# A state buffer with time as its outermost axis, in the S5 recurrence of a hybrid layer

## The chip, the cores and the metric

The kernel runs on one core of one Trainium2 chip. The metric is the device time of one execution in microseconds, with its inputs in the chip's memory. Times of the profile are in microseconds unless marked ns.

## The reference, cut to what matters

The kernel computes one whole layer on 256 tokens of width 2048 in fp32: a mixer with three branches (gated delta rule, gated linear attention, S5 state space model), a cross-attention and a convolutional feed-forward part. The change touches the S5 branch alone. It has 64 groups with 64 complex states each, that is 4096 complex states, and runs them over 256 steps of time:

```
bu_r = jnp.einsum('bsgh,gph->sbgp', uf, bbr)
bu_i = jnp.einsum('bsgh,gph->sbgp', uf, bbi)
...
_, _, xr, xi = lax.associative_scan(combine, (a_r, a_i, bu_r, bu_i), axis=0)
y = (jnp.einsum('sbgp,ghp->bsgh', xr, c_re.astype(f32))
     - jnp.einsum('sbgp,ghp->bsgh', xi, c_im.astype(f32)))
y = y + d_skip.astype(f32).reshape(S5_GROUPS, S5_GROUP) * uf
```

The scan is the recurrence x(t) = a x(t-1) + b u(t) with a complex factor a for each state. The output is a product of all states with C, plus a skip term.

## The kernel before, in words

**The work as a whole.** TensorE multiplies the 256 tokens by all weight matrices, in fp32 split into a high and a low part. The helper `load_w` (line 199) fetches a weight group of 128 x 1024 values, lets ScalarE round it to its high part `whi` and VectorE subtract to get the low part `wlo` (both line 206). `proj` (line 229) and `proj_tok` (line 269) then issue three matmuls for each piece (lines 212 to 221 and 285 to 287), into PSUM accumulators from a pool of five; `total` (line 223) adds the two halves of an accumulator, by a ScalarE copy (L225) and a VectorE add (L226), and so frees it for the next slab.

**The order of the work.** The small stages (the S5 recurrence, the delta rule `dn_core`, the gated linear attention `gla_core`) are Python generators. After each weight group `pump` (line 148) advances the active generators by as much as their rates (R_S5 = 0.7, R_DN = 1.15, R_GLA = 1.7) allow; each `yield` names the share that the piece issued so far uses up. So the instructions of several stages are interleaved in each engine's queue, and each engine works its queue in order. Weight splits have a higher priority than the rest.

**The S5 core** (`s5_core`, line 905) works in two halves of 128 steps of time. The tile X holds, on each of 128 partitions, the real and imaginary part (axis c, 2) of 32 states (axis n) at 128 times (axis s): 8192 words, with time as the innermost axis. Each half has three stages:

- The input products: 64 fp32 matmuls (line 922; each is recorded twice, once for each pass) into PSUM tiles from a pool of three, and 16 evictions by ScalarE (line 926) of 128 x 512 values into X.
- The recurrence on VectorE: for each time t a multiply of the previous states, X[:, :, :, t - 1], by the tile M of factors, into `mm` (line 932, 128 values a partition), an add of the two parts of `mm` into `s_` (line 933, 64 values), and an add of `s_` to X[:, :, :, t] in place (line 934, 64 values). In the first half the first time needs no step, so there are 255 steps. Between the halves the last state is copied into the tile `carry` (line 937), which the first step of the second half reads.
- The output products: 64 fp32 matmuls (line 947; again each recorded twice) with the columns of C as weights and X[:, c, n, :], 128 times, as the moving operand; four of them, for four blocks of 32 output rows, go to four column groups of the array. VectorE and ScalarE then apply skip term and GELU (lines 953 to 961).

In profile lines the tile s_ appears as s__868, and f names tiles of the shared pools; su, the S5 input, is one of them.

**Where it lies in time.** The first half's evictions run from 120 to 161 us, its steps from 161 to 465, its output products from 485 to 494. The second half's evictions run from 487 to 564, its steps from about 565 to 821, its output products from 853 to 869. In the same stretches lie the projections of the mixer with the delta rule (to about 490 us) and the gated linear attention (540 to 660 us).

Of the kernel before, what the change touches and what calls it, by code (L numbers as in the profile page):

```python
# [9 lines left out]
F32 = mybir.dt.float32  # L10
# [8 lines left out]
P = 128  # L19
# [69 lines left out]
class Net:  # L89
# [350 lines left out]
    def dn_core(self):  # L440
# [76 lines left out]
        for i in range(1, 32):  # L517
            tv = tmp[:64, :i * i].rearrange("p (c j) -> p c j", c=i)
            nc.vector.tensor_mul(tv, X3[:64, :i, :i], LS[:64, :i, i][:, None, :].broadcast_to([64, i, i]))  # L519
            nc.vector.tensor_reduce(X3[:64, :i, i], tv, axis=AX.X, op=ALU.add)  # L520
            yield 0.14 + i * i * 2 / 960.0
# [295 lines left out]
    def s5_setup(self, brT, biT):  # L817
# [5 lines left out]
        def tl(n):  # L823
            return self.scr()
        self.X = None
        self.side.dma_start(out=self.Bl[0], in_=brT)
# [78 lines left out]
    def s5_core(self, ctr, cti):  # L905
        nc = self.nc
        su = self.su
        carry = self.s5s.tile([P, 2, 32], F32, name="carry")
        m = self.s5s.tile([P, 2, 2, 32], F32, name="mm")
        s = self.s5s.tile([P, 2, 32], F32, name="s_")  # L910
        for hf in range(2):
            X = self.s5p.tile([P, 2, 32, P], F32, name="X", tag="X")
            tk = slice(hf * P, hf * P + P)
            for f2 in range(4):
                for q2 in range(0, 4, QB):
                    pss = [self.mx([P, 2, 2, P]) for _ in range(QB)]
                    for n in range(2):
                        ft = 2 * f2 + n
                        for c in range(2):
                            for q, ps in enumerate(pss, q2):  # L920
                                rs = slice(32 * q, 32 * q + 32)
                                nc.tensor.matmul(ps[:, n, c, :], self.Bl[c][rs, ft, :], su[rs, ft, tk], start=True,  # L922
                                                 stop=True, tile_position=(32 * q, 0))
                    for q, ps in enumerate(pss, q2):
                        p0 = 8 * f2 + q
                        nc.scalar.copy(X[:, :, p0:p0 + 5:4, :].rearrange("p c n s -> p n c s"), ps)  # L926
                    yield 1.0 * QB
            for t in range(P):
                if t == 0 and hf == 0:
                    continue  # L930
                prev = carry if t == 0 else X[:, :, :, t - 1]
                nc.vector.tensor_mul(m, self.M, prev[:, None].broadcast_to([P, 2, 2, 32]))  # L932
                nc.vector.tensor_add(s, m[:, :, 0, :], m[:, :, 1, :])  # L933
                nc.vector.tensor_add(X[:, :, :, t], X[:, :, :, t], s)  # L934
                yield 0.48
            if hf == 0:
                nc.vector.tensor_copy(carry, X[:, :, :, P - 1])
            Ct = [self.tile4().rearrange("p (n o) -> p n o", n=32) for _ in range(2)]
            self.side.dma_start(out=Ct[0], in_=ctr)
            self.side.dma_start(out=Ct[1], in_=cti)  # L940
            for fb in range(2):
                ps = self.mx([P, 4, P])
                for f in range(4):
                    ft = 4 * fb + f
                    for c in range(2):
                        for q in range(4):
                            nc.tensor.matmul(ps[32 * q:32 * q + 32, f, :], Ct[c][:, 4 * ft + q, :],  # L947
                                             X[:, c, 4 * ft + q, :], start=(c == 0), stop=(c == 1),
                                             tile_position=(0, 32 * q))
                sv = su[:, 4 * fb:4 * fb + 4, tk]  # L950
                for f in range(4):
                    ft = 4 * fb + f
                    nc.vector.scalar_tensor_tensor(sv[:, f, :], sv[:, f, :], self.vec[:, V_S5D + ft:V_S5D + ft + 1],
                                                   ps[:, f, :], op0=ALU.mult, op1=ALU.add)
                y2 = self.tile4(512).rearrange("p (f s) -> p f s", f=4)
                nc.scalar.activation(y2, sv, AF.Square)
                nc.vector.tensor_scalar(y2, y2, 0.044715, 1.0, op0=ALU.mult, op1=ALU.add)
                nc.vector.tensor_mul(y2, y2, sv)
                nc.scalar.activation(y2, y2, AF.Tanh, scale=GELU_C)
                nc.vector.tensor_scalar(y2, y2, 1.0, None, op0=ALU.add)  # L960
                nc.vector.tensor_mul(sv, sv, y2)
                yield 3.0
# [612 lines left out]
```

## Time and profile before

| what | value |
|---|---|
| median of 3 runs | 1946.44 us (1944.46 to 3108.89) |
| the profiled execution | 1944.89 us |
| its span, first to last instruction | 1943.1 us |
| granted TensorE clock, mean | 0.991 |
| instructions | 28177 |

The profile is of one execution. Busy times of the engines overlap. TensorE's matmuls are pipelined, and each record is longer than the time until the next one starts; an idle time in brackets after a row is that before its first instruction, with what ended it.

### The profile page before, as it was taken

To read this page: it belongs to the slowest core of one execution; us is meant where nothing else is said; L and a number is where in the kernel's file an instruction comes from. 1 tells how busy PE (TensorE), PEld (TensorE's weight loads), DVE (VectorE), ACT (ScalarE), POOL (GpSimd) and SP (SyncE) were. 2 spreads that over 40 slices of the span, in tenths; PEclk is the share of its full clock that TensorE was granted. 3 is DMA by queue.
4 is the path that set the end of the run, shared out by engine and by line. 5 is a ranking of instruction groups with operands and counts; after the bars stand their busy time and mean duration, and the time that the engine had idled before them with its cause. 6 is when DMAs were issued, how large, how long until landed. Compare 5 with 4: busy or idle time off the path is not lost.

```text
span 1943.1 us, 28177 instructions
## 1 busy us (share of the span) xinstructions
PE 1881.5 (97%) x10440; PEld 1567.1 (81%) x10440; DVE 1419.6 (73%) x2719; ACT 952.3 (49%) x1426; POOL 67.4 (3%) x117
## 2 busy tenths in 40 slices
PE   7989899999999999999999997999999999999997
PEld 6778788777778688878877986888888888888886
DVE  6868999996569999967666856766666666644445
ACT  5655444343564444544454655555555555534442
POOL 0000012020000000000000000000000000000000
PEclk9999999999999999999999998999999999999999
DMA  7535467674445576666576544655566555676664
GB/s 250 175 108 171 147 205 237 187 260 132 125 126 165 180 220 180 213 216 207 184 262 214 176 147 147 215 185 174 184 195 188 188 187 185 202 226 200 199 192 135
DMA packets 107482, 363.93 MB, mean 187 GB/s; under 512 B 12320, under 2 KB 20896, under 8 KB 106832
## 3 DMA queue, kind: packets, MB, share of 16 engines
q1 hardware_dynamic: 97696, 328.32, 54.9%
q0 software_dynamic: 9648, 33.81, 5.2%
q8 instruction: 82, 1.34, 0.3%
q14 instruction: 56, 0.46, 0.1%
HBM read 350.47 MB, written 11.61 MB: 186 GB/s over the span
## 4 chain that ended last, share of the span: by engine, by line
PE 87%; DVE 7%; issue 4%; DMA 1%; ACT 1%; POOL 0%; SPq 0%; DVEq 0%; ACTq 0%; POOLq 0%
PE acc L218 25%; PE acc L219 14%; PE acc L287 13%; PE acc L285 13%; PE acc L286 13%; DVE wlo L206 2%; PE acc L221 2%; PE mx L922 2%; DVE f L519 1%; DVE mm L932 1%; PE mx L183 0%; PE mx L947 0%; PE mx L641 0%; DVE f L520 0%; DMA mch<-in 0%
## 5 line engine op out<-in xcount | busy, mean ns | idle before, releaser
L206 DVE TENSOR_TENSOR wlo<-raw,whi 128x1024 fp32r<-128x1024 f32 (+1 forms) x632 | 752.8, 1194 | 419.9 <-ACT whi L206 417.6
L206 ACT CAST whi<-raw 128x1024 fp32r<-128x1024 f32 (+1 forms) x632 | 646.7, 1029 | 728.7 <-PE acc L286 378.6
L218 PE MATMUL acc<-aa,whi 128*128 128x512 f32 x2085 | 727.1, 401 | 11.6 <-DVE r L226 9.6
L219 PE MATMUL acc<-aa,wlo 128*128 128x256 f32 x2224 | 556.2, 284 | 10.2 <-DVE wlo L206 10.2
L219 PEld LDWEIGHTS acc<-aa,wlo 128*128 128x128 f32 x2224 | 422.6, 190 | 54.6 <-DVE wlo L206 22.1
L218 PEld LDWEIGHTS acc<-aa,whi 128*128 128x128 f32 x2085 | 386.6, 190 | 82.5 <-issue 11.8
L285 PE MATMUL acc<-whi,aa 128*128 128x512 f32 (+1 forms) x704 | 269.8, 384 | 0.0
L286 PE MATMUL acc<-whi,aa 128*128 128x512 f32 (+1 forms) x704 | 268.5, 382 | 0.0
L287 PE MATMUL acc<-wlo,aa 128*128 128x512 f32 (+1 forms) x704 | 253.3, 385 | 3.7 <-DVE wlo L206 3.6
L287 PEld LDWEIGHTS acc<-wlo,aa 128*128 128x128 f32 x704 | 131.9, 188 | 34.0 <-DVE wlo L206 7.7
L286 PEld LDWEIGHTS acc<-whi,aa 128*128 128x128 f32 x704 | 132.4, 188 | 26.4 <-issue 1.1
L285 PEld LDWEIGHTS acc<-whi,aa 128*128 128x128 f32 x704 | 132.3, 188 | 26.1 <-issue 1.2
L285 PE MATMUL acc<-whi,ach 128*128 128x512 f32 x352 | 136.9, 389 | 0.0
L286 PE MATMUL acc<-whi,acl 128*128 128x512 f32 x352 | 136.9, 389 | 0.0
L287 PE MATMUL acc<-wlo,ach 128*128 128x512 f32 x352 | 123.4, 389 | 0.0
L932 DVE TENSOR_TENSOR mm<-M,X 128x128 f32<-128x128 f32 x254 | 98.6, 388 | 5.4 <-ACT X L926 0.6
L286 PEld LDWEIGHTS acc<-whi,acl 128*128 128x128 f32 x352 | 66.1, 188 | 13.7
L285 PEld LDWEIGHTS acc<-whi,ach 128*128 128x128 f32 x352 | 66.1, 188 | 13.7
L287 PEld LDWEIGHTS acc<-wlo,ach 128*128 128x128 f32 x352 | 66.0, 188 | 13.7
L934 DVE TENSOR_TENSOR X<-X,s__868 128x64 f32<-128x64 f32 x255 | 71.4, 280 | 4.5
L933 DVE TENSOR_TENSOR s__868<-mm 128x64 f32<-128x64 f32 x255 | 56.4, 221 | 4.7
L226 DVE TENSOR_TENSOR r<-r,acc 128x256 f32<-128x256 f32 x143 | 56.9, 412 | 0.7 <-ACT r L225 0.6
(454 smaller groups left out, 1866.9 us busy)
## 6 DMA issues: line engine op xcount, KB each, us to landing
raw<-in SPq DMA_DIRECT2D x600, 512.0 KB, 4.0
raw<-in SPq DMA_DIRECT2D x32, 256.0 KB, 2.7
gd<-r POOLq DMA_DIRECT2D x24, 256.0 KB, 4.5
f<-gd POOLq DMA_DIRECT2D x12, 512.0 KB, 4.9
f<-Rd POOLq DMA_DIRECT2D x4, 512.0 KB, 6.9
f<-in POOLq DMA_DIRECT2D x4, 512.0 KB, 3.7
gp<-in POOLq DMA_DIRECT2D x8, 256.0 KB, 4.5
xn<-in POOLq DMA_DIRECT2D x1, 2048.0 KB, 10.3
```

Source lines behind the costliest of these rows:

```text
L206: self.last = (nc.scalar.copy(hi, raw), self.seq(lambda: nc.vector.tensor_sub(lo, raw, hi.bitcast(F32))))
L218: nc.tensor.matmul(two, hi, x, start=start, stop=False)
L219: nc.tensor.matmul(two[:, 0, :], lo, x[:, 0, :], start=False, stop=False)
L221: nc.tensor.matmul(two, hi, x, start=start, stop=True)
L226: self.nc.vector.tensor_add(r, r, acc[:, 0:T])
L285: nc.tensor.matmul(accs[t], xh[:, ts_], hi[:, kk, :], start=(kt == 0), stop=False)
L286: nc.tensor.matmul(accs[t], xl[:, ts_], hi[:, kk, :], start=False, stop=False)
L287: last[:] = [nc.tensor.matmul(accs[t], xh[:, ts_], lo[:, kk, :], start=False, stop=(kt == KT - 1))]
L922: nc.tensor.matmul(ps[:, n, c, :], self.Bl[c][rs, ft, :], su[rs, ft, tk], start=True, stop=True, tile_position=(32 * q, 0))
L932: nc.vector.tensor_mul(m, self.M, prev[:, None].broadcast_to([P, 2, 2, 32]))
L933: nc.vector.tensor_add(s, m[:, :, 0, :], m[:, :, 1, :])
L934: nc.vector.tensor_add(X[:, :, :, t], X[:, :, :, t], s)
```

## The change

X is allocated with time as its outermost free axis: [time, part, state] in place of [part, state, time]. The number of words, the pool and the buffer stay. Every access to X is rewritten for the new layout: the evictions write it through a permuted view, the recurrence reads and writes X[:, t], and the output products read X[:, :, c, n]. The numbers, order and arithmetic of the instructions in the program text and the amounts that each `yield` names are the same.

```diff
-            X = self.s5p.tile([P, 2, 32, P], F32, name="X", tag="X")
+            X = self.s5p.tile([P, P, 2, 32], F32, name="X", tag="X")
...
-                        nc.scalar.copy(X[:, :, p0:p0 + 5:4, :].rearrange("p c n s -> p n c s"), ps)
+                        nc.scalar.copy(X[:, :, :, p0:p0 + 5:4].rearrange("p s c n -> p n c s"), ps)
...
-                prev = carry if t == 0 else X[:, :, :, t - 1]
+                prev = carry if t == 0 else X[:, t - 1]
                 nc.vector.tensor_mul(m, self.M, prev[:, None].broadcast_to([P, 2, 2, 32]))
                 nc.vector.tensor_add(s, m[:, :, 0, :], m[:, :, 1, :])
-                nc.vector.tensor_add(X[:, :, :, t], X[:, :, :, t], s)
+                nc.vector.tensor_add(X[:, t], X[:, t], s)
...
-                nc.vector.tensor_copy(carry, X[:, :, :, P - 1])
+                nc.vector.tensor_copy(carry, X[:, P - 1])
...
-                                             X[:, c, 4 * ft + q, :], start=(c == 0), stop=(c == 1),
+                                             X[:, :, c, 4 * ft + q], start=(c == 0), stop=(c == 1),
```

## Rows read from the trace of the kernel before

**Rows 1.** The page, busy time, share of the span and instructions of each engine.
```profile
PE 1881.5 (97%) x10440; PEld 1567.1 (81%) x10440; DVE 1419.6 (73%) x2719; ACT 952.3 (49%) x1426; POOL 67.4 (3%) x117
```
**Rows 2.** The page, the chain that ended last, by engine and by line.
```profile
PE 87%; DVE 7%; issue 4%; DMA 1%; ACT 1%; POOL 0%; SPq 0%; DVEq 0%; ACTq 0%; POOLq 0%
PE acc L218 25%; PE acc L219 14%; PE acc L287 13%; PE acc L285 13%; PE acc L286 13%; DVE wlo L206 2%; PE acc L221 2%; PE mx L922 2%; DVE f L519 1%; DVE mm L932 1%; PE mx L183 0%; PE mx L947 0%; PE mx L641 0%; DVE f L520 0%; DMA mch<-in 0%
```
**Rows 3.** Windows: stretch and length, busy time by engine, clock, DMA share, GB/s.
```profile
core 0: us, PE busy (x) PEld busy (x) DVE busy (x) ACT busy (x) POOL busy (x), PEclk, DMA share, GB/s
100.00:161.00 61.00, 55.73 (x351) 47.36 (x351) 41.59 (x84) 32.98 (x54) 0.00 (x0) 0.94 0.43 128
161.00:300.00 139.00, 132.54 (x722) 112.00 (x721) 132.41 (x331) 68.39 (x101) 7.73 (x11) 0.99 0.58 175
363.00:400.00 37.00, 33.36 (x141) 25.68 (x140) 37.00 (x47) 13.62 (x14) 1.66 (x4) 1.00 0.63 191
570.00:600.00 30.00, 26.59 (x270) 22.14 (x270) 29.24 (x60) 13.41 (x22) 0.00 (x0) 0.89 0.43 132
660.00:822.00 162.00, 162.00 (x819) 134.32 (x818) 154.44 (x378) 77.84 (x110) 6.89 (x12) 1.00 0.67 208
```
**Rows 4.** TensorE's waits for VectorE (total, times, longest): 161-300, 300-465, 465-600 us.
```profile
PE acc L218 <- DVE r L226: 4.4, 5, 1.6
...
PE mx L398 <- DVE f L393: 2.1, 1, 2.1
...
PE acc L287 <- DVE wlo L206: 3.6, 6, 1.3
...
PE acc L218 <- DVE r L226: 2.0, 1, 2.0
...
PE acc L218 <- DVE s__868 L933: 1.4, 1, 1.4
```
**Rows 5.** The recurrence's groups of instructions, then L932's form that reads the carry tile.
```profile
L932 DVE TENSOR_TENSOR mm<-M,X 128x128 f32<-128x128 f32 x254 | 98.6, 388 | 5.4 <-ACT X L926 0.6
L934 DVE TENSOR_TENSOR X<-X,s__868 128x64 f32<-128x64 f32 x255 | 71.4, 280 | 4.5
L933 DVE TENSOR_TENSOR s__868<-mm 128x64 f32<-128x64 f32 x255 | 56.4, 221 | 4.7
...
L932 DVE TENSOR_TENSOR mm<-M,carry x1: 293/293/293, 465.1 to 465.1; 128x128 f32<-128x128 f32 x1
```
**Rows 6.** Windows of L932 alone: stretch and length, VectorE busy (steps), clock, DMA.
```profile
161.00:171.20 10.20, 2.32 (x6) 1.00 0.35 103
188.90:197.80 8.90, 1.91 (x5) 1.00 0.39 117
215.50:226.50 11.00, 1.90 (x5) 1.00 0.32 93
324.00:396.40 72.40, 7.22 (x19) 1.00 0.64 196
568.00:586.00 18.00, 0.73 (x2) 0.89 0.48 147
```
**Rows 7.** The output products: all of L947, then TensorE's timeline: start, us, instructions.
```profile
L947 PE MATMUL mx<-X,f x256: 272/273/297, 485.2 to 868.5; 128*32 128x128 f32 x128
...
490.87 3.27 PE L947 MATMUL mx<-X,f 128*32 128x128 f32 x112
494.07 0.50 PE L287 MATMUL acc<-wlo,aa 128*128 128x512 f32 x1
```
**Rows 8.** Two VectorE instructions of the delta rule with a strided source.
```profile
L524 DVE COPY f<-f 64x1024 f32<-64x1024 f32 x1 | 1.1, 1117 | 0.0
...
L519 DVE TENSOR_TENSOR f<-f,f 64x961 f32<-64x961 f32 x1 | 1.9, 1935 | 0.0
```
**Rows 9.** ScalarE's evictions: all of L926, then its timeline before the first step.
```profile
L926 ACT COPY X<-mx x32: 567/586/591, 120.3 to 563.3; 128x512 f32<-128x512 f32 x32
...
159.55 1.70 ACT L926 COPY X<-mx 128x512 f32<-128x512 f32 x3 [0.16 <-PE mx L922]
```

## The prediction

> **What bounds the kernel now.** I read the busy shares first, then the chain that ended last, then both by stretch. TensorE is busy for 1881.5 of 1943.1 us, VectorE for 1419.6 [rows 1]; the chain is 87% PE and 7% DVE, and the recurrence's multiply is in it with 1%, L947 with 0% [rows 2]. The average hides that VectorE is nearly full while the recurrence runs: 132.4 us of 139 from 161 to 300, all 37 us from 363 to 400, 29.2 of 30 from 570 to 600, 154.4 of 162 from 660 to 822 [rows 3]. In the last of these TensorE is busy for all 162 us too, so there the full VectorE holds nobody up. So the question is not how much VectorE work the change removes but how long TensorE stands still for VectorE. The waits answer it: from 161 to 300 it waits 4.4 us for L226 (the sum that frees an accumulator) and 2.1 us for L393; from 300 to 465, 3.6 us for weight splits (L206); from 465 to 600, 2.0 us for L226 and 1.4 us for a recurrence step [rows 4]. Together 13.5 us. That is the most that a faster recurrence can return by the waits, however much VectorE time it saves.
>
> **The recurrence's steps.** Their number, order and arithmetic stay; only the step between elements changes, from 512 bytes (128 words) to 4. The multiply L932 takes 388 ns where it reads X, and 293 ns in the one execution that reads the contiguous carry tile, with the same shape: 95 ns is the price of the strided read. The add L934 reads and writes X strided and takes 280 ns; L933, with the same 64 elements and contiguous output, takes 221 ns: 59 ns [rows 5]. So VectorE is spared 254 x 95 + 255 x 59 ns = 24.1 + 15.0 = 39 us, 154 ns a step. The lower end is 0 (only one row shows the contiguous form), the upper 48 us, if L934 pays the 95/128 ns an element on its read and again on its write and so loses 95 ns too. I take 39, the rows' own differences.
>
> **What of that reaches the end.** A wait of TensorE becomes shorter by the steps that VectorE runs since it last had to wait itself, since what is saved before such a wait is lost in it. At the slab ends at 171, 197 and 226 us, VectorE's last own wait lies at most 11 us back (the stretches in rows 6 begin at those waits); 6, 5 and 5 steps lie in those run-ups. Between 324 and 396 it never waits, and 19 steps lie there. Before the waits at 580 and 586 only 2 do; the dense work there is that of the gated linear attention [rows 6]. At 154 ns a step this is 0.9 + 0.8 + 0.8 + 2.9 + 0.3 = 5.7 us, each part below the wait that it shortens. The ends are 0 (other waits take their place) and 13.5 us (all of [rows 4]). From 570 to 600 the granted clock is 0.89 [rows 3]: part of the stretch runs at the lower of the two levels, 1.2 GHz, which costs about 0.11 x 30 = 3.3 us against 2.4 GHz; the engine had stood still for VectorE before that. If the shorter wait spares it that, 3.3 us more are gained; I leave it out of the sum and in the range. From 600 to 870 I cost the gain at nothing: TensorE is full there without the recurrence being late for it.
>
> **The output products, L947.** This is the new cost, and it stands on the path. The moving operand X[:, c, n, :] was 128 contiguous words; now each word lies 256 bytes from the one before. In the trace 112 matmuls start at 490.87 and the next matmul at 494.07 [rows 7]: four run side by side on the four column groups, so 28 groups take 3.20 us, 114 ns a group, 0.89 ns a column. All 256 are 64 groups, some 7.3 us now. No row shows a TensorE read at such a step. The lower end is 0. It isn't idle talk: a VectorE copy with one source read at a 128-byte step does 1024 elements in 1117 ns [rows 8], 1.09 ns each, not far above TensorE's 0.89, so a reader of one stream at this pace may lose little. The upper end by the same kind of rows is that the four streams of a group are fetched in turn, each with the multiply's 95 ns: 256 x 95 = 24.3 us. The nearest row by access is the multiply itself [rows 5]: 128 elements, one strided stream, 95 ns more. Taken once for each group of four (they have run side by side so far) it gives 64 x 95 = 6.1 us, all exposed: the matmuls before and after these blocks follow without a gap and nothing else runs in their place. I take 6.1.
>
> The Trainium skill (Advanced Engine Details and Errata, SBUF Cachelines) says that successive accesses in one 16-byte line run at full rate and that one line per access is penalised. The multiply's 388 against 293 ns agrees for VectorE; for TensorE no run here shows it. By that rule the lower end of 0 falls away, without a size. The Trainium skill (Vector Engine (DVE) Microarchitecture Reference, Measured stream behaviour) gives 1.73 ns an element for far hops and 2.50 for a step of 24 words, against 1.054; as an estimate from that page, TensorE at the larger price would pay 64 x 128 x 1.45 ns = 11.9 us in place of 6.1, and the sum would be 1952.
>
> **The evictions, L926.** 32 ScalarE copies of 512 elements from PSUM, 586 ns each, now write at a step of 256 bytes. Nearest row for an element priced by its stride: 95 ns / 128 = 0.74 ns; so up to 0.38 us each, 12 us of ScalarE in all, and 0 at the lower end. ScalarE is busy for 33.0 of the 61 us in which the first half's evictions lie [rows 3] and is 1% of the chain [rows 2]; its idle time hides nearly all of it. Not hidden is the end of the first half: three evictions stand back to back at 159.55 [rows 9], the first recurrence step waits for the last of them, and behind that step in VectorE's queue wait L226 and the splits that the slab end at 171 needs. I take 3 x 0.38 = 1.1 us, ends 0 and 2. In the second half the last eviction starts at 563.3 [rows 9] and the steps only some 5 us later. The carry copy and the buffers' size don't change, and there is no DMA in the change.
>
> **The sum,** against the profiled execution's own 1944.89 us (span 1943.1 and 1.8 around it; the median of the runs shown, 1946.44, is 1.6 above): -5.7 + 6.1 + 1.1 = +1.5, so 1946.4 us. No change that could be measured.
>
> **Rivals.**
> (a) TensorE reads the steps as fast as contiguous words. For it: a column takes 0.89 ns and the strided one-stream copy 1.09. Against it: the 95 ns of the multiply. Then -5.7 + 0 + 1.1, 1940.3 us, chance 0.28.
> (b) Slower: the four side-by-side streams of L947 share one path into the array and pay in turn, 24.3 us, in blocks whose neighbours follow them without a gap. For it: four streams at once ask for four words in 0.89 ns, which one word per access makes four accesses. Against it: with contiguous words the four show no queueing that the trace would tell, and the multiply's price was measured for one stream. -5.7 + 24.3 + 1.1 gives 1964.6 us. It decides from the point where a group costs over 72 ns more (4.6 us for the 64), since then the gain is gone. Chance 0.18.
> (c) The same, but each access at the whole 1.9 to 2.0 ns an element that the two-source multiply L519 with a strided operand shows (1935 ns for 961 [rows 8]): 4 x 128 x 1.9 = 0.97 us a group in place of 0.114, 64 x 0.86 = 55 us, 1995 us. Chance 0.05.
> (d) The whole 39 us reaches the end, since VectorE is the true limit wherever it is full: 1944.89 - 39 + 7.2 = 1913 us. Against it: rows 3 and 4, 13.5 us of waits. Chance 0.04. A little over 2% needs all of it and a free L947.
> (e) The multiply stays at 388 ns, because the cost lies in the broadcast of its operand and not in the stride: then only costs are left, 1952 us. Against it: the carry row has the same broadcast. Chance 0.03.
> The forecast itself has 0.42.
>
> **How the numbers follow.** 1946.4 is the likeliest case. The range takes in (a) with the larger gain of the waits and of the clock, down to 1932, and (b), up to 1966; (c), (d) and the far ends lie outside. Two per cent are 39 us, about what a measurement of this kernel can tell from no change: only (d) comes near that on the fast side, 0.03, only (c) and a dearer (b) on the slow side, 0.06, and 0.91 stays within.
>
> **What would show it.** L932 near 293 ns, L934 near 221, VectorE's busy time near 1380 us: the first step right. TensorE's waits for VectorE down from 13.5 to about 8 us: the second. A group of L947 at about 209 ns: the third; at 114 it is (a), near 494 (b). L926 at up to 965 ns without TensorE waiting for L926: the fourth. It is wrong if another order of instructions comes out of the build, or if a wait for L926 or X stands where L226 stood.

## The result, and the profile after

The changed kernel takes 1957.65 us (median of 4 runs, 1956.75 to 1960.56) against 1945.45 before (median of 4): ratio 1.0068, 95% interval [1.0055, 1.0082], some 13 us slower. One of the four runs before took 3108.89 us; the ratio leaves it out. The forecast was 1946.4 and no change; the time lies between the forecast and rival (b). The instructions stand in the same order on every engine in both kernels, so each difference of time comes from how long instructions take and who waits.

The page after: busy time, and the chain by engine and by line.
```profile
PE 1897.4 (97%) x10440; PEld 1576.4 (81%) x10440; DVE 1395.9 (71%) x2719; ACT 982.2 (50%) x1426; POOL 67.4 (3%) x117
...
PE 85%; DVE 7%; issue 4%; DMA 2%; ACT 2%; POOL 0%; DVEq 0%; SPq 0%; ACTq 0%; POOLq 0%
PE acc L218 24%; PE acc L219 13%; PE acc L287 13%; PE acc L285 13%; PE acc L286 13%; DVE wlo L206 2%; PE acc L221 2%; PE mx L922 1%; PE mx L947 1%; DMA raw<-in 1%; DVE f L519 1%; PE mx L183 1%; ACT whi L206 0%; PE mx L641 0%; DVE f L520 0%
```
Against [rows 1, 2], VectorE is busy 24 us less, ScalarE 30 us and TensorE 16 us more (VectorE's saving is 40 us and the evictions' price 16; the last section has the rest). L932 has left the list of the chain's lines, and L947 has come up from 0% to 1%. That is the whole story in small: a cost on an engine that was seldom waited for was exchanged for one on the engine that sets the end.

The recurrence's groups after, the counterpart of [rows 5].
```profile
L932 DVE TENSOR_TENSOR mm<-M,X 128x128 f32<-128x128 f32 x254 | 73.2, 288 | 6.5 <-ACT X L926 1.8
L934 DVE TENSOR_TENSOR X<-X,s__868 128x64 f32<-128x64 f32 x255 | 56.4, 221 | 4.5
```
The multiply falls by 100 ns and the add by 59: 25.4 + 15.0 = 40 us of VectorE time.

TensorE's waits for VectorE after (total, times, longest), from 161 to 300, 300 to 465 and 465 to 600 us, the counterpart of [rows 4].
```profile
PE acc L218 <- DVE X L934: 2.6, 2, 1.4
...
PE mx L398 <- DVE f L393: 1.7, 1, 1.7
...
PE acc L218 <- DVE r L226: 1.1, 3, 0.6
...
PE acc L287 <- DVE wlo L206: 2.4, 4, 1.1
...
PE acc L218 <- DVE s__868 L933: 2.2, 1, 2.2
...
PE acc L218 <- DVE r L226: 1.9, 1, 1.9
```
They come to 11.9 us where they were 13.5. Of 40 us saved on VectorE, 1.6 us show in these waits. The rows understate it, since each of TensorE's records is longer than the time until the next one starts, so that an idle stretch shows only a part of a delay. Measured by the start of the same matmul, the first 16 of the output products begin at 480.41 us in place of 485.19. Of these 4.8 us, 1.5 were there at 161 us, before the first step, so the steps gave back 3.3. A stretch where an engine is full is no stretch where it is waited for.

The output products after, in TensorE's timeline (start, us, instructions), the counterpart of [rows 7].
```profile
487.68 10.66 PE L947 MATMUL mx<-X,f 128*32 128x128 f32 x112
498.27 0.51 PE L287 MATMUL acc<-wlo,aa 128*128 128x512 f32 x1
...
876.01 5.94 PE L947 MATMUL mx<-X,f 128*32 128x128 f32 x62
881.88 0.50 PE L285 MATMUL acc<-whi,aa 128*128 128x512 f32 x1
```
The block of 112 begins 3.2 us earlier than before (487.68 against 490.87) and ends 4.2 us later (498.27 against 494.07). 28 groups now take 10.59 us, 378 ns each, where they took 114. By the end of the last block the lead has become a lag of 13.2 us: in the kernel before, the matmul after it started here.
```profile
866.83 1.95 PE L947 MATMUL mx<-X,f 128*32 128x128 f32 x62
868.70 0.50 PE L285 MATMUL acc<-whi,aa 128*128 128x512 f32 x1
```
The span's end lies 13.2 us later too (1956.3 against 1943.1); after 882 us nothing more is lost or gained on balance.

The evictions after, ScalarE's timeline and then VectorE's before the first step, the counterpart of [rows 9].
```profile
158.01 2.91 ACT L926 COPY X<-mx 128x512 f32<-128x512 f32 x3 [0.15 <-PE mx L922]
...
160.95 0.29 DVE L932 TENSOR_TENSOR mm<-M,X 128x128 f32<-128x128 f32 x1 [1.84 <-ACT X L926]
```
Three evictions take 2.91 us in place of 1.70, and the first step waits 1.84 us for the last of them. In [rows 5] all waits of L932 for L926 were 0.6 us.

### The profile page after: what moved, and what is told of

The parts are those of the page before. It is cut to its first block, busy times and chain, and to the rows that moved or that the text cites. A ratio compares the mean times of both kernels' runs of the same rounds, so it can differ in the third digit from the quotient of the medians.

```text
span 1956.3 us, 28177 instructions
## 1 busy us (share of the span) xinstructions
PE 1897.4 (97%) x10440; PEld 1576.4 (81%) x10440; DVE 1395.9 (71%) x2719; ACT 982.2 (50%) x1426; POOL 67.4 (3%) x117
## 4 chain that ended last, share of the span: by engine, by line
PE 85%; DVE 7%; issue 4%; DMA 2%; ACT 2%; POOL 0%; DVEq 0%; SPq 0%; ACTq 0%; POOLq 0%
PE acc L218 24%; PE acc L219 13%; PE acc L287 13%; PE acc L285 13%; PE acc L286 13%; DVE wlo L206 2%; PE acc L221 2%; PE mx L922 1%; PE mx L947 1%; DMA raw<-in 1%; DVE f L519 1%; PE mx L183 1%; ACT whi L206 0%; PE mx L641 0%; DVE f L520 0%
## 5 line engine op out<-in xcount | busy, mean ns | idle before, releaser
L206 ACT CAST whi<-raw 128x1024 fp32r<-128x1024 f32 (+1 forms) x632 | 662.6, 1054 | 723.0 <-PE acc L286 366.5
L932 DVE TENSOR_TENSOR mm<-M,X 128x128 f32<-128x128 f32 x254 | 73.2, 288 | 6.5 <-ACT X L926 1.8
L934 DVE TENSOR_TENSOR X<-X,s__868 128x64 f32<-128x64 f32 x255 | 56.4, 221 | 4.5
```

The source lines that it names most:

```text
L206: self.last = (nc.scalar.copy(hi, raw), self.seq(lambda: nc.vector.tensor_sub(lo, raw, hi.bitcast(F32))))
L934: nc.vector.tensor_add(X[:, t], X[:, t], s)
```

## The experiments

The theory after the result: the output products' strided reads cost some 17 us on TensorE's path, the recurrence gives back 4 or 5, and the evictions, though nearly twice as long, cost nothing. Rival 1: the evictions, 16 us more of ScalarE, are the loss, and L947's blocks are long because something else is late. Rival 2: the recurrence's new pace has made other waits. In the first four runs Z is the same buffer seen in the other layout, so that one of the three accesses can have its old or new stride alone. The words met are then not the ones meant, and in two of the runs one small copy a half keeps the first step behind the last eviction.

**Recurrence alone.** The change, with the evictions and the output products on contiguous words.
```diff
-nc.scalar.copy(X[:, :, :, p0:p0 + 5:4].rearrange("p s c n -> p n c s"), ps)
+nc.scalar.copy(Z[:, :, p0:p0 + 5:4, :].rearrange("p c n s -> p n c s"), ps)
...
-X[:, :, c, 4 * ft + q], start=(c == 0)
+Z[:, c, 4 * ft + q, :], start=(c == 0)
```
Expected: 

> The recurrence reads and writes contiguous words as in the change, but the evictions write and the output products read the same buffer in their old contiguous way (the words they meet are not the ones meant; one small copy a half keeps the first step behind the last eviction). Theory (the output products' strided reads cost all the loss, and the recurrence gives some microseconds): 1940 to 1942 us, ratio 0.997 to 0.999, a group of L947 at 114 ns. Rival 1 (the strided evictions are the loss): also about 1941. Rival 2 (the loss comes with the recurrence's new pace, through other waits): above 1950.

Measured: 1940.01 us against 1944.40, ratio 0.9978 [0.9968, 0.9988]: 4.3 us faster. Rival 2 falls.

**Output products alone.** The kernel before, with this edit.
```diff
-X[:, c, 4 * ft + q, :], start=(c == 0)
+Z[:, :, c, 4 * ft + q], start=(c == 0)
```
Expected: 

> The kernel before, with only the output products reading at a step of 64 words (other words than meant). Theory: before plus 17 to 18 us, 1962 to 1964, ratio about 1.009, a group of L947 at 380 to 410 ns. Rival 1 (evictions): no change, ratio 1.000, and L947's blocks long only where something else is late. Rival 2: no change.

Measured: 1961.28 us against 1944.40, ratio 1.0089 [1.0075, 1.0102]: 17 us slower. TensorE's timeline of this run:
```profile
490.72 10.83 PE L947 MATMUL mx<-X,f 128*32 128x128 f32 x112
501.48 0.50 PE L287 MATMUL acc<-wlo,aa 128*128 128x512 f32 x1
```
10.76 us for 28 groups is 384 ns a group, with the evictions and the recurrence as they were. Rival 1 falls here already. For the whole, 64 groups times 264 to 270 ns more is 17 us, what the run shows.

**Evictions alone.** The kernel before, with the evictions writing Z at the new stride; the recurrence so meets other words.
```diff
-nc.scalar.copy(X[:, :, p0:p0 + 5:4, :].rearrange("p c n s -> p n c s"), ps)
+nc.scalar.copy(Z[:, :, :, p0:p0 + 5:4].rearrange("p s c n -> p n c s"), ps)
```
Expected: 

> The kernel before, with only the evictions writing at a step of 64 words (and the one small copy a half that keeps the first step behind them). Theory: an eviction takes 1.1 us in place of 0.59, and that is hidden: ratio 0.999 to 1.001, at most 1 us. Rival 1: most of the 13 us, ratio 1.005 or more. Rival 2: 1.000.

Measured: 1945.14 us against 1944.40, ratio 1.0000 [0.9991, 1.0009]. The group of evictions in this run:
```profile
L926 ACT COPY X<-mx 128x512 f32<-128x512 f32 x32 | 33.6, 1097 | 5.7 <-PE mx L922 5.6
```
1097 ns against 586: 16 us more of ScalarE, and below 2 us of it reaches the end.

**The change without the output products' part.**
```diff
-X[:, :, c, 4 * ft + q], start=(c == 0)
+Z[:, c, 4 * ft + q, :], start=(c == 0)
```
Expected: 

> The change, with only the output products put back to contiguous reads (other words than meant). Theory: the loss is gone and the gain of the recurrence stands: 1940 to 1942 us, ratio 0.997 to 0.999 to the kernel before. Rival 1 (evictions): still 1955 or more. Rival 2: still 1955 or more.

Measured: 1942.47 us against 1944.40, ratio 0.9986 [0.9977, 0.9995]: 2.7 us faster. The sign holds; the gain is a little smaller than the recurrence's alone. The first step waits 1.2 us longer for its evictions here, which would fit, but the two intervals overlap and don't prove it.

Together: +17.3 for the output products, -4.3 for the recurrence and 0 for the evictions make +13.0 us by the ratios; the change shows +13.2. The parts add up.

**Why 264 ns a group, and not 95?** That was the term of the forecast that was off, so the next runs ask what TensorE pays for. First, one stream at a time: the same matmuls, issued column group by column group, so that they don't run four side by side, once in the kernel before and once in the change.
```diff
-for f in range(4):
-    for c in range(2):
-        for q in range(4):
+for q in range(4):
+    for f in range(4):
+        for c in range(2):
```
Expected, contiguous: 

> The kernel before, with the output products issued column group by column group, so that 16 matmuls in a row go to the same column group and don't run side by side. Both theories: contiguous words at 0.89 ns a column, 114 ns for each matmul, 256 x 114 = 29 us in place of 7.3 to 10.

Expected, strided: 

> The change, with the same order as in the run above. If four strided streams side by side share one path at about 0.74 ns a word (378 ns for 512 words), one stream alone needs 95 ns for its 128 words, less than the 114 ns that its columns take: as long as in the run above, 114 ns a matmul, 1957 + 11 to 20 us. If each stream alone is slowed to 2.95 ns a word, 378 ns a matmul, 97 us in all and some 70 us more than the run above.

TensorE's timelines, contiguous and then strided, each first to a cut inside one column group and then for the whole block:
```profile
491.00 1.17 PE L947 MATMUL mx<-X,f 128*32 128x128 f32 x9
...
491.00 10.88 PE L947 MATMUL mx<-X,f 128*32 128x128 f32 x124
501.81 1.15 PE L922 MATMUL mx<-f,bl 32*128 32x128 f32 x8
```
```profile
491.53 2.34 PE L947 MATMUL mx<-X,f 128*32 128x128 f32 x10
...
491.53 20.95 PE L947 MATMUL mx<-X,f 128*32 128x128 f32 x124
512.41 0.82 PE L922 MATMUL mx<-f,bl 32*128 32x128 f32 x5
```
The whole blocks take 10.81 and 20.88 us for 124 matmuls, 87 and 168 ns each. These means are not the time of one stream: at each change of column group the last matmuls of one group and the first of the next run in pairs, side by side. Inside one column group the matmuls start 109 ns apart with contiguous words (the first 133) and 217 ns apart with strided ones. So the 114 ns of the first expectation is about right for one stream, though not for the block, and neither branch of the second holds: a single strided stream isn't hidden, it pays 108 ns for its 128 words. One run each, 1972.2 and 1985.8 us; side by side is better in either layout. So the price of one stream was close to VectorE's 95 ns, and what failed was how four of them add up.

**Which steps are dear?** The kernel before, with another step in each of the four blocks of output products; Zf is the buffer as one row of words. The four streams of a group start 123, 119, 7 and 95 words apart at steps of 2, 4, 60 and 16.
```diff
-X[:, c, 4 * ft + q, :], start=(c == 0)
+Zf[:, (32 * c + 4 * ft + q) * w_:(32 * c + 4 * ft + q) * w_ + 127 * st + 1:st], start=(c == 0)
```
Expected: 

> The kernel before, with each of the four blocks of output products reading at another step (other words than meant): 2 and 4 words in the first half, 60 and 16 in the second; a block has 16 groups of four. If a read is priced by 16-byte lines (two words of a line are enough), step 2 takes 114 ns a group and steps 4, 16 and 60 all about 380. If it is priced by pairs of neighbouring words, step 2 too takes about 380. If the price at 64 words comes from words that fall into the same bank, step 60 (an odd number of lines) is clearly below 380.

TensorE's timeline in the first half: a cut of the block before 492.0, all in steps of 2 words, then what is left after 492.0, nearly all in steps of 4, is the rest of the block of 112, up to 495.68.
```profile
490.65 1.61 PE L947 MATMUL mx<-X,f 128*32 128x128 f32 x46
...
490.65 5.10 PE L947 MATMUL mx<-X,f 128*32 128x128 f32 x112
495.68 0.50 PE L287 MATMUL acc<-wlo,aa 128*128 128x512 f32 x1
```
And in the second half, steps of 60 words, then of 16:
```profile
855.52 3.46 PE L947 MATMUL mx<-X,f 128*32 128x128 f32 x54
858.90 0.50 PE L285 MATMUL acc<-whi,aa 128*128 128x512 f32 x1
...
870.78 3.88 PE L947 MATMUL mx<-X,f 128*32 128x128 f32 x62
874.59 0.50 PE L285 MATMUL acc<-whi,aa 128*128 128x512 f32 x1
```
At 2 words 46 matmuls start within 1.35 us: 117 ns a group, nearly as good as contiguous (114). At 4 words the other 66 take 3.68 us, 223 ns a group; at 60 words 54 take 3.38 us, 250 ns; at 16 words 62 take 3.81 us, 246 ns. So two words in a 16-byte line cost next to nothing and one word in each line about doubles the time; the 380 that the expectation put at these steps didn't come, and 64 words, at 378, are a case of their own. Which of step or starting points makes it so, the next run asks.
```diff
+Zf[:, wq * q + wf * ft + wc * c:wq * q + wf * ft + wc * c + 127 * st + 1:st], start=(c == 0)
```
Expected: 

> The kernel before, with the four blocks of output products reading at steps of 64, 64, 60 and 60 words (other words than meant). In the first and third the four streams of a group start one word apart, as in the change; in the second and fourth 16 words apart. If the extra price of 64 over 60 words lies in the step itself, 380, 380, 250 and 250 ns a group; if it lies in four streams that ask for the same line or bank at once, the first and third are dear (380) and the second and fourth cheap (250).

TensorE's timeline, steps of 64 words, up to 497.0 and then the whole block; last, steps of 60 words with starts one word apart:
```profile
492.36 4.99 PE L947 MATMUL mx<-X,f 128*32 128x128 f32 x46
...
492.36 9.08 PE L947 MATMUL mx<-X,f 128*32 128x128 f32 x112
501.37 0.50 PE L287 MATMUL acc<-wlo,aa 128*128 128x512 f32 x1
...
862.81 3.46 PE L947 MATMUL mx<-X,f 128*32 128x128 f32 x54
866.20 0.50 PE L285 MATMUL acc<-whi,aa 128*128 128x512 f32 x1
```
With the four streams one word apart 46 matmuls take 4.64 us, about 400 ns a group; 16 words apart the other 66 take 4.37 us, 265 ns on average (the first few groups still run at the slower pace, and nine in the middle start 216 to 220 ns apart). At 60 words both starts gave 250. So the extra price needs both, a step of 64 words and streams that start one word apart. At a step of 60 words such streams share a line as well, so sharing a line is not enough by itself. Why 60 words are spared, these runs don't tell.

**The same, with the right words.** That gives a cure inside the change: store the states column group by column group, so that the streams of a group start 8 words apart.
```diff
-nc.scalar.copy(X[:, :, :, p0:p0 + 5:4].rearrange("p s c n -> p n c s"), ps)
+nc.scalar.copy(X[:, :, :, 8 * q + 2 * f2:8 * q + 2 * f2 + 2].rearrange("p s c n -> p n c s"), ps)
...
-X[:, :, c, 4 * ft + q], start=(c == 0)
+X[:, :, c, 8 * q + ft], start=(c == 0)
...
+[nc.vector.tensor_copy(m[:, i].rearrange("p c (q f) -> p c f q", q=4), self.M[:, i].rearrange("p c (f q) -> p c f q", q=4)) for i in range(2)]; nc.vector.tensor_copy(self.M, m)
```
Expected: 

> The change, with the states of each part stored column group by column group, so that the four streams of a group of output products start 8 words apart in place of one (the factors M are put in the same order by three small copies). If the extra price at a step of 64 words lies in streams that ask for the same line, a group takes 250 to 270 ns in place of 380: 7 us less than the change, about 1950, ratio to the kernel before 1.003. If it lies in the step alone: 1957, ratio 1.007.

Measured: 1948.10 us against 1946.25, ratio 1.0009 [1.0000, 1.0018]. TensorE's timeline:
```profile
487.99 6.29 PE L947 MATMUL mx<-X,f 128*32 128x128 f32 x112
494.21 0.50 PE L287 MATMUL acc<-wlo,aa 128*128 128x512 f32 x1
```
222 ns a group, below what was expected: 156 ns less on 64 groups are 10 us, and the ratio moved from 1.0068 to 1.0009, 11 us. Inside the block the groups start 218 ns apart, as the matmuls of one strided stream alone do (217): with these starts the four pay the price once, together. Most of the loss came of four streams starting one word apart. That the unit is the 16-byte line is argued and not shown: at this step starts of 1, 8 and 16 words were run, none between.

**Layouts between the two.** If a line of 16 bytes is the unit, two neighbouring times innermost should please everybody: the recurrence then finds two words of each line, and so do the products.
```diff
-X = self.s5p.tile([P, 2, 32, P], F32, name="X", tag="X")
+X = self.s5p.tile([P, P // 2, 2, 32, 2], F32, name="X", tag="X")
...
+prev = carry if t == 0 else X[:, (t - 1) // 2, :, :, (t - 1) % 2]
```
The other accesses follow, and each eviction becomes two of 256 words.

Expected: 

> A third layout: two neighbouring times innermost, so that the recurrence steps by 2 words and the output products read runs of 2 words. If lines of 16 bytes decide, the recurrence stays at 290 and 221 ns and L947 pays for half as many lines, 190 ns a group, +5 us: 1944 us, ratio 1.000. If pairs of neighbouring words decide, L947 stays at 114 ns but the recurrence's reads are priced (388 ns): ratio 1.000 too, told apart by the rows; if both come cheap, 1941 us, ratio 0.998.

Four times innermost are the control; there each step of the recurrence touches one word a line.

Expected: 

> Four neighbouring times innermost: the recurrence steps by 4 words (a new 16-byte line for each), the output products read runs of a whole line. If lines decide, the recurrence is priced again (about 390 and 280 ns) and L947 is at 114 ns a group: no change to the kernel before, ratio 0.999 to 1.001. If a small step is cheaper for VectorE than 128 words, between that and the pairs' 0.998.

Pairs: 1939.68 us against 1944.96, ratio 0.9978 [0.9969, 0.9987]. Quads: 1943.65 against 1944.97, ratio 0.9992 [0.9983, 1.0002]. The 190 ns a group and the ratio of 1.000 that were expected of pairs if lines alone decide didn't come; quads came as expected by lines. Two instructions of the recurrence (shortest, median and longest, ns) and TensorE's timeline at the output products, for pairs and then the same for quads:
```profile
L934 DVE TENSOR_TENSOR X<-X,s__868 x255: 206/225/253, 165.2 to 817.0; 128x64 f32<-128x64 f32 x128
L932 DVE TENSOR_TENSOR mm<-M,X x254: 271/292/309, 164.7 to 815.2; 128x128 f32<-128x128 f32 x127
```
```profile
486.42 4.25 PE L947 MATMUL mx<-X,f 128*32 128x128 f32 x112
490.60 0.50 PE L287 MATMUL acc<-wlo,aa 128*128 128x512 f32 x1
```
```profile
L934 DVE TENSOR_TENSOR X<-X,s__868 x255: 250/273/287, 164.1 to 821.1; 128x64 f32<-128x64 f32 x128
L932 DVE TENSOR_TENSOR mm<-M,X x254: 366/390/416, 163.4 to 819.4; 128x128 f32<-128x128 f32 x127
```
```profile
490.60 3.26 PE L947 MATMUL mx<-X,f 128*32 128x128 f32 x112
493.80 0.50 PE L287 MATMUL acc<-wlo,aa 128*128 128x512 f32 x1
```
A step of 16 bytes costs VectorE as much as one of 512 (390 and 273 ns), a step of 8 bytes next to nothing (292 and 225, against 288 and 221 contiguous). L947 is at 114 ns a group with quads and at 149 with pairs, where two streams of a group share each line. The last run therefore puts both findings together, pairs with the states in the order of the column groups.

Expected: 

> The pairs' layout with the same order of the states. If two streams in one line are what raised a group from 114 to 149 ns, it falls back to about 115 to 120: 2 us less than pairs, 1938 us, ratio 0.997. If not: as pairs, 0.998.

Measured: 1938.70 us against 1946.25, ratio 0.9965 [0.9952, 0.9979], the lowest ratio here, though its interval overlaps that of pairs: 6.8 us ahead of the kernel before and 20 us ahead of the change. Its output products:
```profile
485.01 3.29 PE L947 MATMUL mx<-X,f 128*32 128x128 f32 x112
488.23 0.50 PE L287 MATMUL acc<-wlo,aa 128*128 128x512 f32 x1
```
3.22 us for 28 groups: 115 ns, as contiguous.

## Why the prediction was wrong, point by point

- **What bounds the kernel: right.** The sum goes by what TensorE waits for and does. The 40 us that VectorE was spared moved the end by 4.3 us (recurrence alone), and rival (d), the whole saving, is out.
- **The recurrence's steps: right.** 95 and 59 ns were forecast, 100 and 59 came; rival (e) falls with that. The one row of the carry tile was a fair sample.
- **What reaches the end: right in size, in part by luck.** 5.7 us were forecast, 4.3 measured with an interval of 2.3 to 6.2. The waits were to fall from 13.5 to about 8 us and fell to 11.9: from 161 to 300 only from 6.5 to 5.4, from 300 to 465 from 3.6 to 2.4, and after 465 they rose from 3.4 to 4.1, where 0.3 less was forecast. By the starts of the same matmuls the change gained 0.7 us from 161 to 300, where 2.5 were forecast, and 2.6 from 300 to 465, where 2.9 were. TensorE's clock moves the total by as much: in the trace of the recurrence alone the matmuls are 6.0 us ahead of the kernel before at 484 us and 2.9 ahead at 495, since from 481.4 to 488.2 the granted clock is 0.50, the lower level; the kernel before has such a stretch from 227.0 to 230.4 (0.51) that this run lacks. From 570 to 600 the granted clock rose from 0.89 to 0.94 in the change, without a gain: the same matmuls lie 4.2 us behind at 570 and 4.1 at 600.
- **The evictions: the exposure right, their length not.** 0.38 us more was the upper bound and 0.51 came (1.10 us each). The first step waits 1.2 us longer, as the 1.1 us of the sum had it; in total nothing can be measured.
- **The output products: the step that failed.** Two sentences of the prediction carried it: the multiply's 95 ns "taken once for each group of four (they have run side by side so far) it gives 64 x 95 = 6.1 us". The price of one stream was near the truth, 108 ns against 95. But a group paid 264 ns, 17 us in all, in place of 6.1: its four streams start one word apart, and at this step they then hold each other up. With 8 words between them a group pays 108 ns, as one stream alone, near what the prediction took; so its rule of once for a group held for starts that the change doesn't have. The upper bound, four times 95 or 24.3 us, held, and so did the decision point of rival (b): over 72 ns a group the change loses.
- **The Trainium skill's rule** on 16-byte lines (Advanced Engine Details and Errata, SBUF Cachelines), cited against the lower end of 0, is borne out for TensorE too: 117 ns a group at two words a line, 223 to 250 at one. It says nothing of streams side by side, which made the larger part. By the figures of the Trainium skill (Vector Engine (DVE) Microarchitecture Reference, Measured stream behaviour) the estimate was 11.9 us, nearer to 17 than the term taken. The Trainium skill's rule in that section, that full rate needs runs of at least two adjacent words, doesn't hold for the recurrence's multiply here: single words at a step of two take 292 ns, against 288 for contiguous ones.

## What to carry to other kernels

A layout has a reader on each engine; cost the change for all of them, and begin with the engine that sets the end. An fp32 buffer that two engines read along different axes need not favour one: two words of the other axis innermost made both reads as fast as contiguous ones here, once the four streams of a group also started 16 words apart. Where matmuls run side by side on column groups with a strided moving operand, don't let the operands start in neighbouring words; 8 words between them were enough here.

## What the runs showed of the hardware that was not expected

While the streams that start one word apart ran, ScalarE and VectorE took six to seven times as long for a cast and a subtraction on other tiles than X. ScalarE's and then VectorE's timeline of the change, during the block of L947 that runs from 487.68 to 498.27:
```profile
486.42 1.05 ACT L206 CAST whi<-raw 128x1024 fp32r<-128x1024 f32 x1 [0.17 <-PE acc L286]
487.79 7.34 ACT L206 CAST whi<-raw 128x1024 fp32r<-128x1024 f32 x1 [0.32 <-PE acc L286]
...
487.50 6.95 DVE L206 TENSOR_TENSOR wlo<-raw,whi 128x1024 fp32r<-128x1024 f32 x1
...
499.67 1.22 DVE L206 TENSOR_TENSOR wlo<-raw,whi 128x1024 fp32r<-128x1024 f32 x1
```
The same cast takes 1.05 and 7.34 us, the same subtraction 6.95 and 1.22. The longest cast by run (the three numbers are the shortest, median and longest in ns): the change, the output products alone, and the change with streams 8 words apart.
```profile
L206 ACT CAST whi<-raw x632: 601/1052/7336, 6.7 to 1935.8; 128x1024 fp32r<-128x1024 f32 x152, 128x512 fp32r<-128x512 f32 x6
```
```profile
L206 ACT CAST whi<-raw x632: 601/1052/6243, 7.4 to 1939.1; 128x1024 fp32r<-128x1024 f32 x152, 128x512 fp32r<-128x512 f32 x6
```
```profile
L206 ACT CAST whi<-raw x632: 600/1053/1099, 7.2 to 1926.2; 128x1024 fp32r<-128x1024 f32 x152, 128x512 fp32r<-128x512 f32 x6
```
With 8 words between the starts the long casts are gone too. So such streams cost the other engines' instructions as well. In the pages' busy times this is 8.6 us of VectorE and 17.6 of ScalarE (1395.9 and 982.2 in the change, 1387.3 and 964.6 with the streams 8 words apart). The rest of the gap between VectorE's 40 us saved and the 24 us of the page is there without the strided output products too (1387.5 in the change without them, 32 less than before): VectorE's records overlap, and an overlap counts once as busy time. No run was made to tell whether TensorE's 378 ns a group is itself lengthened by the two engines' accesses.

Further:

- One contiguous stream alone took 109 ns a matmul from start to start, and four side by side took no more for a group (109, 114 with the ends of the block). One strided stream alone took 217 ns; four side by side 218 a group (222 with the ends) when they started 8 words apart, and 378 when one word apart.
- The extra price showed at a step of 64 words and not at 60 (about 400 against 250 ns a group, with the same starting points). The cause stays open. Nor is it paid by every group: in the change's last block the first three groups start 218 to 264 ns apart, with the same step and starts, and the later ones 347 to 589.
- ScalarE's evictions from PSUM went from 586 to 1100 ns for 512 words written at a step of 256 bytes, 1.0 ns a word, more than the 0.74 ns that a strided read costs VectorE's multiply.
